# Scores of the second attention by row halves: three products of 64 rows for each head, two heads side by side

## The chip, the cores and the metric

The kernel runs on one core of one Trainium2 chip. The metric is the device time of one execution in microseconds; the time before is the median of three runs. A core has five engines that run their own instruction streams and wait for one another by semaphores: PE (the matrix engine; its weight loads are listed apart as PEld), DVE (the vector engine), ACT (the scalar engine), POOL and SP. PE multiplies a stationary operand (up to 128 rows by 128 columns, loaded first) with a moving operand that streams through, and sums into PSUM; DVE and ACT read PSUM and the on-chip memory SBUF.

## The reference

The model is a two-layer encoder over 512 tokens of width 1024. Layer 0 mixes with RWKV-7 and memory cross-attention, layer 1 with chunked attention against a shared K and V and again memory attention; each layer ends in a convolutional GLU. The part that matters here is the chunked attention of layer 1: twelve heads of 64, queries in chunks of 64, each chunk seeing itself and everything up to eight chunks back, which for 512 tokens is a causal mask by chunks.

```python
def one_chunk(c):
    start = c * CHUNK
    qc = lax.dynamic_slice_in_dim(q, start, CHUNK, axis=2)
    kc = lax.dynamic_slice_in_dim(k_pad, start, BAND, axis=2)
    vc = lax.dynamic_slice_in_dim(v_pad, start, BAND, axis=2)
    s = jnp.einsum('bhqd,bhkd->bhqk', qc, kc).astype(jnp.float32) * scale + bias
    kpos = start - PAD_LEN + jnp.arange(BAND)
    s = jnp.where(kpos >= 0, s, neg)
    p = jax.nn.softmax(s, axis=-1).astype(vc.dtype)
    return jnp.einsum('bhqk,bhkd->bhqd', p, vc)
```

Everything is float32. The kernel keeps that accuracy on PE by splitting each operand into a high part in the matrix engine's rounded type (F32R) and the low rest, `x = h + l`, and summing `h*h + h*l + l*h`.

## The kernel before

The second attention stands between the two feed-forward blocks, inside one `ExitStack` (L1718 onward). The twelve heads go as six pairs; a pair's queries, keys or values are one tile of 128 partitions, head 0 on partitions 0 to 63 (`HS[0]`) and head 1 on 64 to 127 (`HS[1]`). The stage's parts are Python generators:

- `q_proj(i)`, `k_proj(i)`, `v_proj(g)` project. `dense` (L250) makes 24 PE products of 512 columns for one tile (L258, L259, L262), `v_proj` 96 products of 256 columns for two pairs (L1805 to L1807). Their weights are loaded and split by `load_w`: a cast on ACT (L208) and a subtraction on DVE (L216).
- `q_split` (L1763) scales the queries on DVE (L1765) and lays them out per head as a **stack** of 128 partitions: in `qs[:, h]` the head's own 64 partitions hold its high part and the other 64 its low part. That takes a cast on ACT (L1769) and a subtraction on DVE (L1770) per head, each over 64 partitions that may lie elsewhere than their source.
- `k_proj` scales the keys (L1780) and makes two tiles, `ks` (the high part of head h on both halves, L1784 and L1785 on ACT) and `kl` (the low part on both halves, L1787 on DVE): four casts and four subtractions over 64 x 512.
- `attention(i)` runs a pair. `rows(hh, qt)` makes the scores of one head for 128 queries and n = 128 (qt + 1) keys by two products of 128 rows (L1827 with `ks`, L1828 with `kl`): the stack sums all the cross terms inside the array, with the low-by-low term besides. Then come the bias and the row maximum on DVE (L1832), the exponential on ACT (L1834), the reciprocal (L1835) and the scaling on DVE (L1836). `turn(hh, qt)` transposes the result on PE in blocks of 128 (L1842) and copies it to `ptT` on ACT (L1844). The eight units (four query blocks by two heads) go in turn, and a unit is transposed after `LAG = 3` further units have had their scores. At the end L1856 multiplies by the values (64 output columns per head), and the result is put aside or split for the output projection.
- The memory attention of the layer (`mem_qk`, `score_b`, L1908 and L1909) uses the same stacked form and is not changed; its queries come from `q_proj` with a name `"m0"` or `"m1"` as `unit`.

Two chains of generators are merged by `weave` (L99): the attentions with the memory attention between the second and third pair, and the projections with the start of the output projection. Every `yield` carries a cost in ns; `weave` always continues the chain that has used the smaller share of its declared total (`ATT_COST`, L1866, for one pair). Conditions such as `after_unit` hold a projection back until an earlier pair is done, since `ks` and `kl` have two buffers, `qs` three, `sb` four, and the PSUM pool of the stage six banks (two more for `dense`). The tile layer then gives every engine its own fixed order, which follows the merged order but may move an instruction past others; the engine works through that order strictly.

Of the kernel before, what the change touches and what calls it, by code (L numbers as in the profile page):

```python
# [18 lines left out]
P = 128  # L19
# [114 lines left out]
def trunk_kernel(ctx, tc, A, out):  # L134
# [1589 lines left out]
    with ExitStack() as bctx:  # L1724
# [38 lines left out]
        def q_split(ps, T):  # L1763
# [4 lines left out]
            for h in range(2):  # L1768
# [4 lines left out]
        def k_proj(i, T, ps=None):  # L1773
# [7 lines left out]
            ks = ap_.tile([P, 2, S], F32R, name="ks", tag="ks")  # L1781
            kl = ap_.tile([P, 2, S], F32R, name="kl", tag="kl")
            for h in range(2):
                SC.copy(ks[HS[h], h], k_[HS[h]])  # L1784
                SC.copy(ks[HS[1 - h], h], k_[HS[h]])  # L1785
                for rows_ in HS:
                    V.tensor_tensor(kl[rows_, h], k_[HS[h]], ks[HS[h], h], op=ALU.subtract)  # L1787
            T["k"] = ks, kl
# [22 lines left out]
        def attention(i, T):  # L1811
            yield lambda: "k" in T and i // 2 in vS
            qs, (ks, kl) = T["q"], T["k"]
# [7 lines left out]
            def rows(hh, qt):  # L1821
                n = (qt + 1) * P
                st = ap_.tile([P, 4], F32, name="st", tag="st", bufs=6)
# [3 lines left out]
                PE.matmul(ps[:, :n], qs[:, hh, qc], mix(ks[:, hh, :n]), start=True, stop=False)  # L1827
                PE.matmul(ps[:, :n], qs[:, hh, qc], mix(kl[:, hh, :n]), start=False, stop=True)  # L1828
                yield n * 0.94
                sb = sbs[hh, qt] = ap_.tile([P, S], F32, name="sb", tag="sb", bufs=4)  # L1830

                V.tensor_tensor_reduce(flat_(sb[:, :n]), sorted_(ps[:, :n]), flat_(big[hh][:, S - n:S]), -1.0, 3e38,  # L1832
                                       op0=ALU.add, op1=ALU.min, accum_out=st[:, 0:1])
                SC.activation(sb[:, :n], sb[:, :n], AF.Exp, scale=-1.0, bias=st[:, 0:1], accum_out=st[:, 1:2])  # L1834
                V.reciprocal(st[:, 2:3], st[:, 1:2])  # L1835
                V.tensor_scalar(sb[:, :n], sb[:, :n], st[:, 2:3], None, op0=ALU.mult)  # L1836

            def turn(hh, qt):
                n = (qt + 1) * P
                pst_ = ps_s()  # L1840
# [235 lines left out]
```

## Time and profile before

| | |
|---|---|
| time, median of 3 runs | 1252.66 us (1251.97 to 1254.84) |
| time of the profiled execution | 1255.45 us |
| its span, first to last instruction | 1253.7 us |
| granted TensorE clock | 0.998 |
| PE, DVE, ACT busy over the span | 97%, 82%, 67% |
| second attention, 724 to 894 us: PE, DVE, ACT busy | 163.5, 116.9, 116.7 of 170 us |

The span is 1.75 us shorter than the profiled execution's time. "Busy" is the time in which an instruction is listed as running. On PE neighbouring products overlap in the list: a product is shown for its whole passage through the array, while the next one starts as soon as the columns have been streamed in. So the distance from start to start is the price of a product, and a busy PE can still have lost time. The waits view names what an idle engine waited for; the timeline merges neighbours of one kind (x16 is sixteen of them) and gives the idle time before a row in brackets with what ended it.

### The profile page before, as it was taken

The numbers are of one execution on the slowest core, as the hardware profiler recorded it, in microseconds if no ns is written. First come the engines' busy times: TensorE is split into PE (matmuls) and PEld (weight loads), VectorE is DVE, ScalarE is ACT, GpSimd is POOL, SyncE is SP. The second block draws the span as 40 slices with busy tenths as digits, with TensorE's granted clock in tenths as the row PEclk, the third lists the DMA queues.
The fourth block names the chain that finished last, engine by engine and source line by source line (L and its number), as shares of the span: only waits on it lengthen the run. The fifth ranks groups of instructions, "written<-read, shape, count | busy, mean of one in ns | idle before, by whom it ended". The sixth has DMA issues, their size and how long they took to land.

```text
span 1253.7 us, 26444 instructions
## 1 busy us (share of the span) xinstructions
PE 1219.9 (97%) x10420; PEld 1074.8 (86%) x10420; DVE 1027.6 (82%) x1958; ACT 840.5 (67%) x1396; POOL 150.8 (12%) x180
## 2 busy tenths in 40 slices
PE   8999999999999999999999999999999999999997
PEld 6787777777789999999888878777799999998886
DVE  7976677766679999999886976668799999999785
ACT  6557668765567777776664676767667777765662
POOL 1000000000001223221120000000002222221300
PEclk9999999999999999999999999999999999999999
DMA  6356354354063999995995332234428999978961
GB/s 210 97 170 131 82 116 96 80 110 104 19 202 92 205 207 217 208 201 140 307 223 144 99 113 68 85 109 135 130 56 189 206 214 212 202 167 259 257 169 67
DMA packets 95293, 191.10 MB, mean 152 GB/s; under 512 B 22080, under 2 KB 30400, under 8 KB 95168
## 3 DMA queue, kind: packets, MB, share of 16 engines
q1 hardware_dynamic: 68592, 129.14, 32.3%
q0 software_dynamic: 26576, 60.26, 27.7%
q8 instruction: 82, 1.34, 0.4%
q14 instruction: 43, 0.35, 0.1%
HBM read 173.15 MB, written 6.29 MB: 143 GB/s over the span
## 4 chain that ended last, share of the span: by engine, by line
PE 66%; DVE 14%; ACT 8%; DMA 7%; issue 4%; POOL 0%; SPq 0%; DVEq 0%; ACTq 0%; POOLq 0%
PE psf L453 11%; PE psf L735 7%; PE psf L455 6%; PE psf L461 4%; PE psd L262 4%; PE psd L258 4%; PE psd L259 4%; PE psf L740 4%; PE psd L735 3%; PE psf L466 2%; DVE wlo L216 2%; PE psd L740 2%; DMA tmp<-r2h 1%; DMA tmp<-r1h 1%; PE pss L1856 1%
## 5 line engine op out<-in xcount | busy, mean ns | idle before, releaser
L529 ACT CAST whi<-raw 128x1024 fp32r<-128x1024 f32 (+1 forms) x168 | 150.3, 937 | 22.6 <-PE psf L453 19.6
L208 ACT CAST whi<-wraw 128x1024 fp32r<-128x1024 f32 x84 | 87.3, 1045 | 63.7 <-PE psd L259 33.9
L453 PE MATMUL psf<-tl,whi 128*128 128x256 f32 x512 | 121.5, 275 | 0.1
L453 PE MATMUL psf<-th,whi 128*128 128x256 f32 x512 | 121.3, 276 | 0.0
L534 DVE TENSOR_TENSOR wlo<-raw,whi 128x1024 fp32r<-128x1024 f32 (+1 forms) x108 | 108.9, 1010 | 0.0
L258 PE MATMUL psd<-r1h,whi 128*128 128x512 f32 x264 | 104.1, 395 | 0.0
L259 PE MATMUL psd<-r1l,whi 128*128 128x512 f32 x264 | 101.7, 386 | 0.0
L453 PEld LDWEIGHTS psf<-tl,whi 128*128 128x128 f32 x512 | 98.4, 192 | 0.5 <-DVE tl L276 0.5
L453 PEld LDWEIGHTS psf<-th,whi 128*128 128x128 f32 x512 | 98.2, 192 | 0.1
L216 DVE TENSOR_TENSOR wlo<-wraw,whi 128x1024 fp32r<-128x1024 f32 x67 | 81.6, 1218 | 19.0 <-ACT whi L208 18.5
L725 ACT CAST whi<-raw 128x1024 fp32r<-128x1024 f32 (+1 forms) x52 | 49.4, 950 | 51.1 <-PE psf L735 27.4
L726 DVE TENSOR_TENSOR wlo<-raw,whi 128x1024 fp32r<-128x1024 f32 (+1 forms) x52 | 56.4, 1096 | 28.3 <-ACT whi L725 24.9
L501 POOL DMA_DIRECT2D wlv<-in_ffn_in_dram x40 | 48.2, 1204 | 250.7 <-ACT wlv L500 187.5
L455 PE MATMUL psf<-th,wlo 128*128 128x256 f32 x504 | 77.1, 276 | 0.0
L556 ACT ACTIVATE tmp<-tmp,vec 128x512 f32<-128x512 f32 x44 | 36.0, 818 | 58.2 <-DVE tmp L543 58.2
L262 PE MATMUL psd<-r1h,wlo 128*128 128x512 f32 x264 | 70.3, 389 | 0.0
L455 PEld LDWEIGHTS psf<-th,wlo 128*128 128x128 f32 x504 | 66.4, 192 | 0.0
L258 PEld LDWEIGHTS psd<-r1h,whi 128*128 128x128 f32 x264 | 49.8, 189 | 9.1 <-issue 2.0
L259 PEld LDWEIGHTS psd<-r1l,whi 128*128 128x128 f32 x264 | 49.9, 189 | 6.4 <-issue 0.7
L262 PEld LDWEIGHTS psd<-r1h,wlo 128*128 128x128 f32 x264 | 47.9, 189 | 6.8 <-issue 0.3
L516 DVE TENSOR_TENSOR raw<-raw 128x1024 f32<-128x1024 f32 x42 | 51.1, 1217 | 0.0
L258 PE MATMUL psd<-r2h,whi 128*128 128x512 f32 x128 | 50.3, 394 | 0.5 <-ACT r2h L1706 0.3
(622 smaller groups left out, 3741.1 us busy)
## 6 DMA issues: line engine op xcount, KB each, us to landing
raw<-in_ffn_in_dram SPq DMA_DIRECT2D x42, 512.0 KB, 5.1
raw<-in_ffn_in_dram SPq DMA_DIRECT2D x84, 256.0 KB, 5.6
wlv<-in_ffn_in_dram POOLq DMA_DIRECT2D x40, 512.0 KB, 7.7
raw<-in_ffn_out_dram SPq DMA_DIRECT2D x30, 512.0 KB, 6.3
raw<-in_ffn_out_dram POOLq DMA_DIRECT2D x24, 512.0 KB, 9.9
wraw<-in_wA_dram SPq DMA_DIRECT2D x20, 512.0 KB, 4.1
wraw<-in_w_out_dram SPq DMA_DIRECT2D x16, 512.0 KB, 4.2
wraw<-in_ffn_outp_dram SPq DMA_DIRECT2D x16, 512.0 KB, 5.6
```

Of the source, the lines that this page charges most:

```text
L208: high = lambda: pin(SC.copy(hi[:, :n], raw))
L216: pin(V.tensor_tensor(lo[:, :n], raw, hi[:, :n], op=ALU.subtract))
L258: PE.matmul(ps, wh[:, j * P:(j + 1) * P], ah, start=start and n == 0, stop=False)
L259: dense_at[0] = PE.matmul(ps, wh[:, j * P:(j + 1) * P], al, start=False, stop=False)
L262: dense_at[0] = PE.matmul(ps, wl[:, j * P:(j + 1) * P], moving(act(k))[0], start=False, stop=stop and n == len(ks) - 1)
L453: PE.matmul(ps, wh[:, o + k * P:o + k * P + P], x[k][n], start=k == n == 0, stop=False)
L455: PE.matmul(ps, wl[:, ol + k * P:ol + k * P + P], x[k][0], start=False, stop=k == 3)
L529: keep(SC.copy(hi[:, :n], self.pair(what) if n > S else self.raw[:, what]))
L534: keep(V.tensor_tensor(lo[:, :n], self.pair(what) if n > S else self.raw[:, what], hi[:, :n], op=ALU.subtract))
L726: V.tensor_tensor(lo, s_, hi, op=ALU.subtract)
L735: PE.matmul(ps[:], a[:, k0 + i, ts], woven(hi[:, i * S:i * S + S]), start=bool(first) and (first is True or t in first) and a is act[0] an ...
L740: PE.matmul(ps[:], act[0][:, k0 + i, ts], woven(lo[:, i * S:i * S + S]), start=False, stop=bool(last) and t in last and i == n - 1)
```

## The change

Queries and keys of the six attention pairs are no longer stacked. `split_to` (L274: one ACT cast, one DVE subtraction, over all 128 partitions) writes the high parts of both heads into `qs[:, 0]` and `ks[:, 0]`, the low parts into `qs[:, 1]` and `ks[:, 1]`; each head stays on its own 64 partitions. `kl` goes from this path. The stacked branch stays for the memory attention.

The scores of a head are now three products that use only the head's 64 rows: high by high, high by low, low by high. `rows(qt)` handles both heads: the loop over the parts is outside and the heads alternate inside, each head summing into a PSUM bank of its own. `turn(qt)` transposes both heads, and a query block is transposed after the next block's scores. The yields and `ATT_COST` change with that.

```diff
+        PARTS = (0, 0), (0, 1), (1, 0)
...
-            q_split(ps, T)
+            q_split(ps, T, unit is not None)
...
+            if not stacked:
+                split_to(qs[:, 0], qs[:, 1], q[:])
+            for h in range(2) if stacked else ():
                 SC.copy(qs[HS[h], h], q[HS[h]])
                 V.tensor_tensor(qs[HS[1 - h], h], q[HS[h]], qs[HS[h], h], op=ALU.subtract)
...
-            ks = ap_.tile([P, 2, S], F32R, name="ks", tag="ks")
-            kl = ap_.tile([P, 2, S], F32R, name="kl", tag="kl")
-            for h in range(2):
-                SC.copy(ks[HS[h], h], k_[HS[h]])
-                SC.copy(ks[HS[1 - h], h], k_[HS[h]])
-                for rows_ in HS:
-                    V.tensor_tensor(kl[rows_, h], k_[HS[h]], ks[HS[h], h], op=ALU.subtract)
-            T["k"] = ks, kl
+            ks = T["k"] = ap_.tile([P, 2, S], F32R, name="ks", tag="ks")
+            split_to(ks[:, 0], ks[:, 1], k_[:])
...
-            def rows(hh, qt):
+            def rows(qt):
...
-                ps = ps_s()
-                qc = slice(qt * P, (qt + 1) * P)
-                PE.matmul(ps[:, :n], qs[:, hh, qc], mix(ks[:, hh, :n]), start=True, stop=False)
-                PE.matmul(ps[:, :n], qs[:, hh, qc], mix(kl[:, hh, :n]), start=False, stop=True)
-                yield n * 0.94
+                pss = [ps_s() for _ in range(2)]
+                for a, b in PARTS:
+                    for hh, ps in enumerate(pss):
+                        PE.matmul(ps[:, :n], qs[HS[hh], a, qc], mix(ks[HS[hh], b, :n]), start=a == b, stop=a == 1)
+                yield 2 * n * 0.7
...
-            us = [(hh, qt) for qt in range(4) for hh in range(2)]
-            for n, u in enumerate(us):
-                yield from rows(*u)
-                if n >= LAG:
-                    yield from turn(*us[n - LAG])
-            for u in us[-LAG:]:
-                yield from turn(*u)
+            for qt in range(4):
+                yield from rows(qt)
+                if qt >= 1:
+                    yield from turn(qt - 1)
+            for qt in range(4 - 1, 4):
+                yield from turn(qt)
...
-        ATT_COST = 2 * 1280 * 1.7 + 2300
+        ATT_COST = 2 * 1280 * 1.47 + 2300
```

How this changes the fixed orders is seen at two places. The first is PE at the start of the last pair, behind the value products of the pair before (L1856); `pss<-ks,qs` and `pss<-kl,qs` are scores, `pss<-cst,sb` transposes, `psd` rows belong to the output projection. Before:

```order
L1856 MATMUL pss<-ptT,vS 64x128 x2
L1827 MATMUL pss<-ks,qs 128x128
L1828 MATMUL pss<-kl,qs 128x128
...
L1842 MATMUL pss<-cst,sb 128x128
L1827 MATMUL pss<-ks,qs 128x384
L1828 MATMUL pss<-kl,qs 128x384
L262 MATMUL psd<-r2h,wlo 128x512 x4
L258 MATMUL psd<-r2h,whi 128x512
L1842 MATMUL pss<-cst,sb 128x128
L1827 MATMUL pss<-ks,qs 128x384
L1828 MATMUL pss<-kl,qs 128x384
L1842 MATMUL pss<-cst,sb 128x128 x2
```

And with the change:

```order
L1856 MATMUL pss<-ptT,vS 64x128 x2
L1826 MATMUL pss<-ks,qs 128x128 x6
L1826 MATMUL pss<-ks,qs 128x256 x6
L259 MATMUL psd<-r2l,whi 128x512
L262 MATMUL psd<-r2h,wlo 128x512 x4
L1842 MATMUL pss<-cst,sb 128x128
L262 MATMUL psd<-r2h,wlo 128x512 x2
L1842 MATMUL pss<-cst,sb 128x128
L1826 MATMUL pss<-ks,qs 128x384 x6
L1842 MATMUL pss<-cst,sb 128x128 x4
L1826 MATMUL pss<-ks,qs 128x512 x6
```

The two heads' scores of a query block now stand together as one group of six, and the transposes of the second block's two heads stand together right behind the third block's scores.

The second place is ACT where the keys of the fourth pair are split while the third pair's last blocks are copied out of PSUM. Before:

```order
L1834 ACTIVATE sb,st<-sb,st 128x512
L1844 COPY ptT<-pss 128x3x128
L1784 CAST ks<-tmp 64x512
L1785 CAST ks<-tmp 64x512
L1784 CAST ks<-tmp 64x512
L1785 CAST ks<-tmp 64x512
L1844 COPY ptT<-pss 128x4x128 x2
```

With the change:

```order
L208 CAST whi<-wraw 128x1024
L1833 ACTIVATE sb,st<-sb,st 128x512 x2
L1845 COPY ptT<-pss 128x3x128 x2
L275 CAST ks<-tmp 128x512
L1845 COPY ptT<-pss 128x4x128 x2
```

Ahead of the last two copies, for which the value products wait, there is one cast in the place of four.

More of the change, by code (lines that the diff above doesn't have):

```diff
@@ L1819, in attention @@
             sbs = {}
[L1821 removed]
+            def rows(qt):
                 n = (qt + 1) * P
[L1823 removed]
+                qc = slice(qt * P, (qt + 1) * P)
                 mix, flat_, sorted_ = (woven, halved, plain_order) if qt > 1 else (lambda t: t,) * 3
[L1825 to L1836 removed]
@@ new lines, in turn @@
+            def turn(qt):
+                n = (qt + 1) * P
+                psts = [ps_s() for _ in range(2)]
+                for hh, pst_ in enumerate(psts):
+                    for kt in range(qt + 1):
+                        PE.transpose(pst_[:, kt * P:(kt + 1) * P], sbs[hh, qt][:, kt * P:(kt + 1) * P], C("ident"))
+                yield 2 * n * 0.85
+                for hh, pst_ in enumerate(psts):
+                    SC.copy(pts[hh][:, 0:qt + 1, qt * P:(qt + 1) * P], pst_[:, :n].rearrange("p (a b) -> p a b", b=P))
```

19 lines of the change are left out of this document (10 added, 9 removed).

## The prediction

> **What bounds the kernel now.** First the page: the slices of the span, and the chain that ended last.
>
> ```profile
> PE   8999999999999999999999999999999999999997
> PE 66%; DVE 14%; ACT 8%; DMA 7%; issue 4%; POOL 0%; SPq 0%; DVEq 0%; ACTq 0%; POOLq 0%
> ```
>
> PE is busy in every slice and holds two thirds of the chain. So a microsecond of matrix work added or taken away on PE counts in full, while one on DVE or ACT counts only where PE waits for it. The table by stretches, over the second attention cut by its pairs (first and fifth stretch, and the sum of all seven):
>
> ```profile
> 724.00:754.00 30.00, 27.65 (x185) 23.36 (x184) 23.44 (x56) 22.45 (x49) 0.29 (x2) 1.00 0.32 96
> 826.00:846.00 20.00, 19.39 (x144) 16.49 (x142) 9.77 (x34) 12.02 (x31) 0.33 (x2) 1.00 0.27 93
> sum 170.00, PE 163.51 PEld 130.68 DVE 116.86 ACT 116.67 POOL 1.45; mean PE 23.36 PEld 18.67 DVE 16.69 ACT 16.67 POOL 0.21
> ```
>
> In 170 us PE is idle for 6.5, while DVE and ACT have 53 us to spare each. What PE waits for in 724 to 905 us, from the waits view (total, times, longest):
>
> ```profile
> PE pss L1842 <- DVE st L1835: 1.5, 2, 0.9
> PE pss L1856 <- ACT ptT L1844: 1.4, 3, 0.5
> PE pss L1827 <- ACT ks L1785: 1.1, 2, 0.6
> PE pss L1842 <- DVE sb L1836: 0.7, 3, 0.2
> ```
>
> So PE waits for the softmax (L1842), for the copies ahead of the value products (L1856) and for the split keys (L1827). These waits cap what less work on DVE and ACT can return.
>
> **The change, part by part.** *Less streaming.* Full-array scores from the timeline (start, listed duration):
>
> ```profile
> 757.29 0.27 PE L1828 MATMUL pss<-kl,qs 128*128 128x128 f32 x1
> 757.40 0.33 PE L1827 MATMUL pss<-ks,qs 128*128 128x256 f32 x1
> 757.57 0.28 PE L1828 MATMUL pss<-kl,qs 128*128 128x256 f32 x1
> 757.68 0.38 PE L258 MATMUL psd<-r2h,whi 128*128 128x512 f32 x1
> ...
> 741.25 0.33 PE L1828 MATMUL pss<-kl,qs 128*128 128x384 f32 x1
> 741.41 0.38 PE L258 MATMUL psd<-r1h,whi 128*128 128x512 f32 x1
> ...
> 742.07 0.44 PE L1842 MATMUL pss<-cst,sb 128*128 128x128 f32 x2
> 742.26 0.46 PE L1827 MATMUL pss<-ks,qs 128*128 128x512 f32 x1
> 742.56 0.38 PE L1828 MATMUL pss<-kl,qs 128*128 128x512 f32 x1
> 742.77 0.81 PE L262 MATMUL psd<-r1h,wlo 128*128 128x512 f32 x3
> ```
>
> From start to start a product of 128 columns takes 0.11 us, of 256 0.11, of 384 0.16, of 512 0.21: 0.60 for one product in each of the four query blocks (0.11 + 0.11 + 0.16 + 0.215). A pair made four such sets (two heads, two products), 2.4 us; if the halves run side by side it makes three, 1.8. Six pairs: **-3.6 us**. Do the halves run side by side? No F32R product on 64 rows stands in this trace, but plain f32 ones do: in the first layer L1338 alternates the two halves into two banks, and L1628 stays on one half for a run.
>
> ```profile
> 307.57 1.99 PE L1628 MATMUL pss<-kmT,kn 64*128 64x256 f32 x8
> 85.27 0.38 PE L258 MATMUL psd<-r1h,whi 128*128 128x512 f32 x1
> 85.49 0.38 PE L259 MATMUL psd<-r1l,whi 128*128 128x512 f32 x1
> 85.80 0.60 PE L1338 MATMUL pss<-AR,KB 64*128 64x128 f32 x6
> 85.80 1.16 PE L1338 MATMUL pss<-AR,KB 64*128 64x128 f32 x16
> 86.89 0.48 PE L258 MATMUL psd<-r1h,whi 128*128 128x512 f32 x1
> 87.21 0.38 PE L259 MATMUL psd<-r1l,whi 128*128 128x512 f32 x1
> ```
>
> The run's sixth product of L1338 ends 0.60 after its start and the sixteenth 1.16: five pairs in 0.56, 0.112 a pair. On one half alone, L1628's eight products of 256 columns take 1.99, at most 0.25 each, 0.12 for 128 columns. So a pair costs what one product costs: the halves overlap. These operands stream at about half the F32R pace (512 columns in 0.21 above); that the overlap holds at the full pace is carried over, not seen.
>
> *A switch on each side.* The same rows give the price of leaving the full array and coming back. From 85.49 to 87.21 are 1.72 us: the slots of L259 and L258 (0.216 each, by 85.27 to 85.49) and eight pairs at 0.112 make 1.33. The rest, **0.39 us**, is the switch in and out. Before the change no score pays it: in 742.07 to 742.56 two transposes at 0.11 and a score at 0.215 make 0.435 of the 0.49. In the changed order the scores stand in 24 separate groups (five in the first pair, three in the second, then four, five, four, three, with one or more full-array rows between): 24 x 0.39 = **+9.4 us**. One group follows the value products, whose 64 columns already left the full mode: -0.2. Together with the streaming PE's own work grows by 5.6 us. The bounds: 24 switches of nothing (-3.6), and the switch in full with no overlap of the halves, in which case six products stand where four stood (+3.6 in the place of -3.6), at +12.8.
>
> The Trainium skill speaks against the change too: TensorEngine Tiling, Key Properties, says that a change of the tiling mode, not just of the tile, drains the engine. It gives no price; with none the sum would keep the -3.6, with the rows' 0.39 it is as above.
>
> *Less splitting.* The groups of 724 to 894 us:
>
> ```profile
> L1787 DVE TENSOR_TENSOR kl<-tmp,ks 64x512 fp32r<-64x512 f32 x24 | 16.4, 684 | 0.4
> L1770 DVE TENSOR_TENSOR qs<-tmp,qs 64x512 fp32r<-64x512 f32 x16 | 11.0, 686 | 0.5
> L1769 ACT CAST qs<-tmp 64x512 fp32r<-64x512 f32 x16 | 9.9, 618 | 5.6 <-DVE tmp L1765 5.3
> L1784 ACT CAST ks<-tmp 64x512 fp32r<-64x512 f32 x12 | 7.4, 617 | 2.1 <-DVE tmp L1780 2.0
> ```
>
> Twelve query casts become six (the four for the memory queries stay), 24 key casts become six; the subtractions likewise. A cast over 128 partitions is taken at the same 0.62 us as over 64, as its columns are the same (the bounds are nothing and twice that, which moves a part of the next term). That is 24 x 0.617 = 14.8 us off ACT and 24 x 0.685 = 16.4 off DVE, all beside PE. It pays where PE waited behind these casts. At the start of the stage and ahead of the second pair's value products:
>
> ```profile
> 728.37 0.28 PE L1807 MATMUL pss<-wlo,r1h 128*128 128x256 f32 x1
> 729.25 0.33 PE L1827 MATMUL pss<-ks,qs 128*128 128x128 f32 x1 [0.60 <-ACT ks L1785]
> 729.68 0.38 PE L259 MATMUL psd<-r1l,whi 128*128 128x512 f32 x1
> 730.53 0.33 PE L1827 MATMUL pss<-ks,qs 128*128 128x128 f32 x1 [0.47 <-ACT ks L1785]
> 731.03 0.38 PE L1805 MATMUL pss<-whi,r1h 128*128 128x256 f32 x1 [0.17 <-ACT vS L1809]
> ...
> 749.10 0.38 PE L258 MATMUL psd<-r2h,whi 128*128 128x512 f32 x1
> 750.02 1.12 PE L1856 MATMUL pss<-ptT,vS 128*64 128x512 f32 x3 [0.54 <-ACT ptT L1844]
> ```
>
> Start to start, less the slot of the product ahead, the first place loses 0.77 + 0.63 + 0.39 = 1.8 us. Five of the first ten casts there go, and 71 value products now stand ahead of the first score, not 48: I take all of the 1.8. At 749.10 the loss is 0.92 - 0.215 = 0.70 for 0.54 of listed idle, so a listed wait costs 0.16 more than it shows; the three waits of L1856 cost 1.4 + 3 x 0.16 = 1.9, and three casts less (1.85 us) ahead of those copies cover each of them. Smaller delays of the fourth and fifth pair's keys I put at 0.8. **-4.5 us**; bounds: nothing, and all 6.5 of idle with its 0.16 for each of some 16 waits, -9.
>
> *Heads in step.* The second block's transposes of both heads now follow the third block's scores directly in four pairs, with a little dense work between in two. How late the second head was, in the first pair:
>
> ```profile
> 740.51 0.30 PE L1842 MATMUL pss<-cst,sb 128*128 128x128 f32 x1 [0.57 <-DVE st L1835]
> 742.46 0.35 DVE L1836 TENSOR_SCALAR sb<-sb,st 128x256 f32<-128x256 f32 x1
> ```
>
> Its scaled block was ready at 742.81, 2.3 us after the first transpose. In the new order PE is there after two transposes (0.22), two dense products (0.43) and the 384-column group (0.48 + 0.39): 1.5 us, and waits 0.8. Behind the waiting transposes stand the 512-column scores, and DVE and ACT wait for those. Six times up to 0.8, less what the freed DVE and ACT bring forward: I take **+2.0** (0 to 4.8). Against it, where PE waits for the first block's softmax anyhow (the L1842 rows), the way out of the new group runs inside the wait: 0.2 in each pair, **-1.3** (0 to -2.4).
>
> Sum: 5.6 - 4.5 + 2.0 - 1.3 = **+1.8 us**. The profiled execution took 1255.45 for a span of 1253.7, 2.8 above the median; the term is a difference, so I put it on the median, 1252.66: **1254.5 us**.
>
> **The rivals.**
>
> *The paired transposes wait.* One mechanism, at the transposes of the second block behind the 384-column scores: the full 4.8 us of waits and, PE being late anyway, nothing of the switches hidden: 5.6 - 4.5 + 4.8 = +5.9, 1258.6. It decides from 1.4 us of such waits on (5.6 - 4.5 + 1.4 = 2.5). For it speaks that the lag is shorter by one head and that DVE serves the two heads one after the other; against it, DVE and ACT are each freed of about 9% of the stage.
>
> *The lighter engines win.* PE's waits all but vanish (-9) and the lag costs nothing (0), the switch staying as priced: 5.6 - 9 = -3.4, 1249.3. For it: the longest single waits are behind casts that go. Against it: the two largest left are L1842 behind the softmax's own steps, which stay.
>
> *No overlap at full pace.* The banks or the array take the two F32R streams one after the other: 5.6 + 7.2 - 4.5 + 0.7 = +9.0, 1261.7. The rows above show the overlap at half pace only.
>
> *Loads do not hide.* With three products per half and a new load for each, every pair shows its load. An exposed load is seen in 742.26 to 742.56, 0.30 for a slot of 0.215: 0.085. With 72 pairs this adds 6.1, +7.9, 1260.6. Against it: L1338's pairs, each with its own load, run at 0.112 without a gap. This is the Trainium skill's rule in TensorE: Matmul & The Clock Gate, The mechanism, by which a load overlaps a running product only when the row group differs; the trace disagrees for the f32 pairs.
>
> **How the numbers follow.** About 0.2% (2.5 us) is what a measurement of this kernel can tell from no change. The forecast, within that of the median: 0.40. The paired transposes wait 0.26, no overlap 0.07, loads do not hide 0.05: slower 0.38. The lighter engines win: faster 0.22. The forecast's own range is 1251 to 1257; for 8 in 10 it reaches down past the faster case's 1249.3, and up through the loads' 1260.6 to the no-overlap case: 1248.5 to 1261.5.
>
> **What would show it.** The new score line runs in pairs a few ns apart, 0.215 us a pair at 512 columns; if 0.43, the halves do not overlap. The product ahead of a group and the first behind it stand about 0.39 further apart than the slots between. PE's waits on L1785 are gone and those of the value products on the ptT copies short; the waits of the transposes on L1836's successor are longer. PE's idle time in the stage falls while its busy time rises by about 5 us. The forecast is wrong if a group costs under 0.2 us of switching, or if the transposes' waits fall as well.

## The result, and the profile after

The changed kernel is slower, by about 4 us. It was compared with the kernel before on two occasions, with these medians:

| comparison | with the change | before | ratio, 95% interval |
|---|---|---|---|
| first | 1259.05 us (8 runs, 1256.37 to 1262.19) | 1254.27 us (8 runs) | 1.0030 (1.0015 to 1.0044) |
| again, with the experiments below | 1259.06 us (12 runs) | 1255.58 us (35 runs) | 1.0032 (1.0016 to 1.0048) |

The ratios are those of the record; the quotient of the two medians is 1.0038 and 1.0028. The time lies inside the predicted range of 1248.5 to 1261.5, but the likeliest case, no change at 1254.5, is not what came. The profiled execution took 1257.51 us with a span of 1255.7, against 1255.45 and 1253.7 before: 2.0 us apart.

The attention itself is the first place to look. The chain of the page, then the table by stretches of the changed kernel (columns as before: window, length, PE busy, PEld, DVE, ACT, POOL, granted clock, DMA share, GB/s):

```profile
PE 65%; DVE 15%; ACT 8%; DMA 7%; issue 5%; POOL 0%; SPq 0%; DVEq 0%; ACTq 0%; POOLq 0%
```

```profile
724.00:754.00 30.00, 28.98 (x196) 23.40 (x195) 18.12 (x48) 18.53 (x42) 0.29 (x2) 1.00 0.29 94
826.00:846.00 20.00, 19.61 (x142) 15.96 (x142) 9.85 (x34) 11.06 (x30) 0.29 (x2) 1.00 0.27 93
sum 170.00, PE 164.28 PEld 128.35 DVE 102.58 ACT 101.64 POOL 1.31; mean PE 23.47 PEld 18.34 DVE 14.65 ACT 14.52 POOL 0.19
```

DVE and ACT have lost 14.3 and 15.0 us of work, where 16.4 and 14.8 had been computed. PE is listed as busy for 0.8 us more. What PE waits for in 724 to 905 us:

```profile
PE pss L1842 <- DVE st L1834: 3.2, 5, 1.4
PE pss L1842 <- DVE sb L1835: 1.8, 6, 0.4
PE pss L1803 <- ACT vS L1807: 0.7, 2, 0.5
```

The waits for split keys and those of the value products are gone, and those of the transposes (L1842) for the softmax on DVE have grown from 2.2 to 5.0 us. From PE's first product of the stage's norm (L328) to the first product of the projection's third output tile (the first `psf` row of L258) the kernel before took 177.76 us and the changed one 177.83. So the attention came out even, and the two microseconds are lost later. PE's waits in 893 to 965 us, before and after:

```profile
PE psf L453 <- ACT whi L529: 0.7, 2, 0.4
```

```profile
PE psf L453 <- ACT whi L529: 1.4, 2, 1.0
PE psf L453 <- DVE r1l L317: 0.8, 2, 0.4
PE psf L453 <- ACT r1h L316: 0.5, 1, 0.5
```

These are the first products of the second feed-forward (L453). They now wait for `r1h` and `r1l`, the split of its input. ACT's timeline shows why those are late (in brackets the idle time before a row and what ended it); first before, then with the change:

```profile
908.31 0.70 ACT L887 ACTIVATE tmp<-xT,vec 128x512 f32<-128x512 f32 x1
908.92 1.03 ACT L208 CAST whi<-wraw 128x1024 fp32r<-128x1024 f32 x1
911.17 1.04 ACT L275 CAST th<-sp 128x1024 fp32r<-128x1024 f32 x1 [1.22 <-DVE sp L898]
```

```profile
907.50 0.72 ACT L887 ACTIVATE tmp<-xT,vec 128x512 f32<-128x512 f32 x1
912.74 1.05 ACT L208 CAST whi<-wraw 128x1024 fp32r<-128x1024 f32 x1 [4.52 <-DMA wraw<-in_w_out_dram]
913.69 1.04 ACT L275 CAST th<-sp 128x1024 fp32r<-128x1024 f32 x1
```

ACT stands still for 4.5 us, because the projection's last weight has not landed, and everything behind its cast in ACT's order, the cast to `th` (L275) and the next splits of the input, is later by 2.5 us. The weight is late, to begin with, because it was asked for late. The issues of the three last weight loads on SP, before and after (start, length of the row, count of issues in it):

```profile
895.83 2.06 SPq L227 DMA_DIRECT2D wraw<-in_w_out_dram  x2
902.68 0.33 SPq L227 DMA_DIRECT2D wraw<-in_w_out_dram  x1
```

```profile
895.04 0.33 SPq L227 DMA_DIRECT2D wraw<-in_w_out_dram  x1
901.81 4.21 SPq L227 DMA_DIRECT2D wraw<-in_w_out_dram  x2
```

A load needs a free buffer, and the buffer of the second of the three came free later, because the subtraction that reads it (L216, the split of the projection's fifth weight) went further back in DVE's order. The last load then waits for the sixth weight's subtraction, which comes behind it on DVE. Before, the fifth weight's subtraction follows the sum into `xT` of the second output tile (L426); now it follows that of the third:

```profile
895.72 0.68 DVE L426 TENSOR_TENSOR xT<-xT,psd 128x512 f32<-128x512 f32 x1
896.32 1.22 DVE L216 TENSOR_TENSOR wlo<-wraw,whi 128x1024 fp32r<-128x1024 f32 x1
```

```profile
899.93 0.68 DVE L426 TENSOR_TENSOR xT<-xT,psf 128x512 f32<-128x512 f32 x1
900.53 1.22 DVE L216 TENSOR_TENSOR wlo<-wraw,whi 128x1024 fp32r<-128x1024 f32 x1
```

This makes the request for the last weight 3.0 us later in the timeline (905.69 for 902.68). The load then also takes twice as long to land: 7.0 us (at 912.66) for 3.5 before (at 906.15). Before, it was asked for ahead of two loads that POOL issues; now it comes behind them. Their rows, before and after:

```profile
904.91 1.74 POOL L496 DMA_DIRECT2D tmp<-in_ffn_in_dram  x2 [31.93 <-PE psf L262]
```

```profile
904.15 1.75 POOL L496 DMA_DIRECT2D tmp<-in_ffn_in_dram  x2 [32.88 <-DVE r1l L317]
```

In the changed kernel the second of these lands at 912.48, just ahead of the weight. In the four profiles whose last weight is asked for within 1.6 us of the second POOL load, it takes 5.9 to 7.0 us; in the seven that ask 2.5 to 3.3 us behind it, 4.0 to 5.2. So about half of its lateness is this meeting of loads; that they share the DMA engines is the likely reason, and no run isolates it.

Neither L426 nor L216 is part of the change. The tile layer gives every engine its order for the whole program, and this place came out differently.

### The profile page after: what moved, and what is told of

It is laid out like the page before. It is cut to its first block, busy times and chain, and to the rows that moved or that the text cites. A ratio compares the mean times of both kernels' runs of the same rounds, so it can differ in the third digit from the quotient of the medians.

```text
span 1255.7 us, 26482 instructions
## 1 busy us (share of the span) xinstructions
PE 1221.3 (97%) x10468; PEld 1072.5 (85%) x10468; DVE 1013.1 (81%) x1934; ACT 825.4 (66%) x1372; POOL 150.7 (12%) x180
## 4 chain that ended last, share of the span: by engine, by line
PE 65%; DVE 15%; ACT 8%; DMA 7%; issue 5%; POOL 0%; SPq 0%; DVEq 0%; ACTq 0%; POOLq 0%
PE psf L453 11%; PE psf L735 7%; PE psf L455 6%; PE psf L461 5%; PE psd L258 4%; PE psf L740 3%; PE psd L262 3%; PE psd L259 3%; PE psd L735 3%; PE psf L466 2%; DVE wlo L216 2%; PE psd L740 2%; DMA tmp<-r1h 1%; DMA raw<-in_ffn_in_dram 1%; PE pss L1856 1%
## 5 line engine op out<-in xcount | busy, mean ns | idle before, releaser
L208 ACT CAST whi<-wraw 128x1024 fp32r<-128x1024 f32 x84 | 87.4, 1045 | 73.6 <-PE psd L259 36.8
L453 PE MATMUL psf<-tl,whi 128*128 128x256 f32 x512 | 121.5, 275 | 0.1
L453 PE MATMUL psf<-th,whi 128*128 128x256 f32 x512 | 121.3, 276 | 0.0
L258 PE MATMUL psd<-r1h,whi 128*128 128x512 f32 x264 | 104.7, 397 | 0.0
L216 DVE TENSOR_TENSOR wlo<-wraw,whi 128x1024 fp32r<-128x1024 f32 x67 | 81.7, 1220 | 22.6 <-ACT whi L208 21.1
L453 PEld LDWEIGHTS psf<-tl,whi 128*128 128x128 f32 x512 | 98.3, 192 | 0.5 <-DVE tl L276 0.5
L453 PEld LDWEIGHTS psf<-th,whi 128*128 128x128 f32 x512 | 98.1, 192 | 0.1
L258 PEld LDWEIGHTS psd<-r1h,whi 128*128 128x128 f32 x264 | 49.9, 189 | 9.9 <-issue 2.4
L258 PE MATMUL psd<-r2h,whi 128*128 128x512 f32 x128 | 50.2, 392 | 0.3 <-ACT r2h L1706 0.3
```

Of the source, the lines that this page charges most:

```text
L208: high = lambda: pin(SC.copy(hi[:, :n], raw))
L216: pin(V.tensor_tensor(lo[:, :n], raw, hi[:, :n], op=ALU.subtract))
L258: PE.matmul(ps, wh[:, j * P:(j + 1) * P], ah, start=start and n == 0, stop=False)
L453: PE.matmul(ps, wh[:, o + k * P:o + k * P + P], x[k][n], start=k == n == 0, stop=False)
```

## The experiments

Two theories. *Order at the projection*: the attention is even, and the loss comes from the order that the planner gave to the weights' splits behind it. *Switches*: the loss is PE's own work in the attention. Each kernel has a profile; from each come two lengths that repeat well: the stage as above, and the time from the first to the hundred-and-first product of L453 in the second feed-forward. The rest of the program, the same in all of them, does not repeat as well: the stretch ahead of the stage ended between 714.1 and 718.7 us in the ten profiles of the experiments, without any edit there.

| kernel | stage, us | first hundred of L453, us | time against before, 95% interval |
|---|---|---|---|
| before | 177.76 | 21.69 | |
| the change | 177.83 | 24.33 | 1.0030 (1.0015 to 1.0044) |
| the change again | 177.85 | 24.45 | 1.0032 (1.0016 to 1.0048) |
| early split | 177.92 | 22.14 | 0.9998 (0.9988 to 1.0009) |
| before, late split | 179.59 | 22.40 | 1.0005 (0.9991 to 1.0019) |
| before, late split and late cast | 179.57 | 24.14 | 1.0021 (1.0006 to 1.0036) |
| early split, no alternation | 178.74 | 22.25 | 1.0022 (1.0006 to 1.0037) |
| early split, full rows | 168.11 | 21.63 | 0.9914 (0.9890 to 0.9939) |
| early split, two groups | 177.48 | 22.38 | 0.9982 (0.9969 to 0.9995) |
| the same, more between | 177.89 | 22.03 | 0.9994 (0.9980 to 1.0008) |
| early split, splits put back | 183.36 | 22.87 | 1.0035 (1.0019 to 1.0051) |
| before, heads in step | 177.67 | 21.66 | 0.9992 (0.9978 to 1.0007) |

In the two late variants of the kernel before, 1.6 us of the stage are not theirs: the granted clock fell for a moment (last section).

### The changed kernel with the split early

Only `out_proj` of the second layer differs: the fourth and fifth weight are loaded and split right behind the first two sums, and the two steps of the feed-forward's input behind them are held until the fifth weight's subtraction (`low_at`) has been issued. PE's order is the same as the changed kernel's, row by row.

```diff
+            if m < len(own):
+                ws[m + 3] = load_w(A["w_out"][l, m + 3])
+            with tc.issue_after(low_at[0].ins) if own and m == 1 else ExitStack():
+                for _ in range((0, 2)[m] if m < len(own) else 1):
+                    next(taken)
-            next(taken)
```

> The changed kernel, in which only the order around the output projection of the second layer is another: the fifth weight of the projection is split on DVE (L216) right behind the sum into xT of the second output tile, where the kernel before has it, and not behind the sum of the third. PE's order is the same. Theory 'late weight': the attention itself came out even (PE at the first product L258 of the third output tile at 894.37 before, 894.23 after), and the loss arises because this split is 4.2 us later, which delays the load behind it, then an ACT cast, then the splits of x at the start of the feed-forward. Then the profiled span falls by the 2.0 us of the profiles, to about 1253.7, the 4.5 us wait of ACT for a weight at 912 us and PE's waits for r1h and r1l at 925 to 930 us go, and the time comes back to within 0.2% of the kernel before. Rival 'switches': the loss is that of PE's own work in the attention, and the time stays about 4 us above the kernel before.

Measured: 1256.50 us (12 runs) against 1256.63 (29 runs), 0.9998 (0.9988 to 1.0009). On ACT the last weight's cast now waits 1.2 us, and PE's waits for `r1h` and `r1l` are gone:

```profile
911.41 1.05 ACT L275 CAST th<-sp 128x1024 fp32r<-128x1024 f32 x1 [1.55 <-DVE sp L898]
913.62 1.04 ACT L208 CAST whi<-wraw 128x1024 fp32r<-128x1024 f32 x1 [1.16 <-DMA wraw<-in_w_out_dram]
```

```profile
PE psf L453 <- ACT whi L529: 1.9, 2, 1.1
```

The first hundred products of L453 take 22.14 us, 2.2 less than with the change. The span of this one profile is 1256.4 and did not fall as expected, since the stretches outside scatter by more than that (the stage began at 717.87, not 716.40); the medians did what the theory says. With this order, the change is a change of nothing.

The reason is not the one that was expected. The last weight does not come earlier here: it is asked for at 909.13 and lands at 913.55, which is 17.8 us behind the end of the stage, for 18.4 with the change and 11.8 before. But the edit has also put its cast behind the cast to `th`, as the rows show, and so ACT does not hold `th` back while it waits. In the kernel before and in the changed one the last weight's cast comes first. So two things make the loss together: a last weight that lands late, and a cast of it that stands ahead of the one to `th`. The kernel before has only the second, and the early split only the first.

### The kernel before with the split late

```diff
+        def late_w(src):
+            hi, lo, second = split_w(raw_w(src), 1024, hold=True)
+            with tc.issue_after(add.ins):
+                second()
+            return hi, lo
...
-                nxt = load_w(A["w_out"][l, m + 1]) if m + 1 < KD else None
+                nxt = (late_w if l and m == 3 else load_w)(A["w_out"][l, m + 1]) if m + 1 < KD else None
```

(`add` is the sum into `xT` of the tile before.)

> The kernel before, in which only the split of the fifth weight of the output projection is put behind the sum of the third output tile on DVE, as it stands in the changed kernel; the attention is untouched. 'Late weight': 2 to 4 us slower than the kernel before, ACT waits some 4 us for a weight at about 910 us and PE waits for r1h and r1l at the start of the feed-forward. 'Switches': no change.

Measured: 1256.94 us against 1256.63, 1.0005 (0.9991 to 1.0019): no change, where 2 to 4 us were expected. The load was late as in the changed kernel, but it cost the first hundred of L453 only 0.7 us. So a late split does not cost the loss by itself. The rows show why. Here, too, the cast to `th` stands ahead of the last weight's cast in ACT's order, though the edit did not ask for it, and ACT uses the wait for it:

```profile
914.53 1.05 ACT L275 CAST th<-sp 128x1024 fp32r<-128x1024 f32 x1 [1.39 <-DVE sp L898]
917.63 1.04 ACT L208 CAST whi<-wraw 128x1024 fp32r<-128x1024 f32 x1 [2.05 <-DMA wraw<-in_w_out_dram]
```

### The kernel before with the late split and the late cast

The same, and the second split of the token sums is held until the last weight's cast (`high_at`) has been issued; for that the last weight's load stands earlier in the program. ACT's order is then that of the kernel before again, where the last weight's cast comes first as well (908.92 and 911.17 above):

```diff
+            if l and m == 4:
+                w7 = load_w(A["w_out"][l, 7])
+                with tc.issue_after(high_at[0].ins):
+                    held_th[0]()
             next(taken)
...
-                    split_to(*(t[:, m - 1:m + 1].rearrange("p a s -> p (a s)") for t in (Th, Tl)), su)
+                    th = [t[:, m - 1:m + 1].rearrange("p a s -> p (a s)") for t in (Th, Tl)]
+                    held_th[0] = lambda h=th, u=su: split_to(*h, u)
+                    if l == 0 or m != 3:
+                        held_th[0]()
```

> The kernel before with two things of the changed kernel's order around the projection and nothing of its attention: the fifth weight's split stands late on DVE, and on ACT the cast of the last weight stands ahead of the second split of the token sums (the cast to th, L275), as it does in the changed kernel. 'Order at the projection, both together': the first hundred products of the second feed-forward take 24.3 us as in the changed kernel, not 21.7, and the time rises by 2 to 4 us. If that order is not the cause, no change (0.9991 to 1.0019 with the late split alone).

Measured: 1260.26 us against 1256.77, 1.0021 (1.0006 to 1.0036). ACT's wait is there, in a kernel whose attention nobody touched:

```profile
917.88 1.04 ACT L208 CAST whi<-wraw 128x1024 fp32r<-128x1024 f32 x1 [5.70 <-DMA wraw<-in_w_out_dram]
918.83 1.04 ACT L275 CAST th<-sp 128x1024 fp32r<-128x1024 f32 x1
```

The first hundred of L453 (L457 in this kernel) take 24.14 us, as in the changed kernel. The waits in them are not the same ones: PE waits mostly for the casts of the feed-forward's weights on ACT (1.7 us) and little for `r1l` (0.2), and PE's own order came out another there. A further 1.5 us are lost inside the projection, where PE waits for a weight's split (1.3 us, `whi` of L208); the changed kernel does not lose those.

The time of this kernel is weaker evidence than its lengths. Nine of its twelve runs had a mean granted clock of 0.997 or less; the three at 0.998 or more took 1254.90 to 1257.21 us, in the mean 1256.0, and the kernel before took 1256.1 at such clocks (8 runs). So for the time the cause rests on the early split: another order of the projection takes the loss of the changed kernel away, with PE's order the same. The lengths show it both ways: with a late weight the first hundred take 24.1 to 24.5 us when its cast comes first (the change twice, and this kernel) and 22.1 to 22.4 when it comes second (the early split and the late split); the kernel before has the cast first and the weight in time, 21.7.

### The change again

The kernel of the change, unedited.

> The changed kernel as it is, once more, timed beside the kernel before on the chip of the following runs. 'Order at the projection' (the loss is made at the start of the feed-forward by where the weights' splits came to stand, since the same kernel with the early split measured 0.9998 of the kernel before): again slower by 2 to 5 us, and the profile shows again some 4 us of ACT waiting for a weight near 912 us and 2 to 3 us of PE waits behind 925 us. 'Scatter' (the first comparison was unlucky, and the change was even all along): within 1 us of the kernel before.

Measured: 1.0032 (1.0016 to 1.0048). The first comparison was not unlucky, and the loss does not hang on the clock: in the runs with a mean granted clock of 0.998 or more the change took 1257.8 us (7 runs) and the kernel before 1254.4 (13 runs). ACT's wait is there again, 4.48 us, and so are PE's for `r1l` and `r1h` (1.1 and 0.5):

```profile
910.96 1.05 ACT L208 CAST whi<-wraw 128x1024 fp32r<-128x1024 f32 x1 [4.48 <-DMA wraw<-in_w_out_dram]
```

### Without alternation

On the kernel of the early split, as are the next four.

```diff
-                for a, b in PARTS:
-                    for hh, ps in enumerate(pss):
+                for hh, ps in enumerate(pss):
+                    for a, b in PARTS:
```

> The kernel of the early split, in which the three score products of head 0 stand one behind the other and then the three of head 1: no alternation of the row halves. If the halves overlap at the full pace only when they alternate, a group of scores streams up to five sets where the alternating one streams three: 2 x 0.60 us for each of six pairs, 7.2 us more of PE's own work than with the early split, some of it inside waits: 5 to 8 us slower. If the overlap is worth nothing, no change.

Measured: 1258.44 us against 1256.63, 1.0022 (1.0006 to 1.0037), about 3 us above the early split by the ratios (2 by the medians), where 5 to 8 were expected; the stage is 0.8 us longer. The compiled program has the three products of head 0 and then the three of head 1, and PE does not run them so. A group of six at 512 columns, in PE's timeline of the changed kernel and of this one:

```profile
741.81 0.38 PE L259 MATMUL psd<-r1l,whi 128*128 128x512 f32 x1
742.12 0.92 PE L1826 MATMUL pss<-ks,qs 64*128 64x512 f32 x6
742.96 1.56 PE L262 MATMUL psd<-r1h,wlo 128*128 128x512 f32 x6
```

```profile
740.98 0.38 PE L259 MATMUL psd<-r1l,whi 128*128 128x512 f32 x1
741.29 0.92 PE L1826 MATMUL pss<-ks,qs 64*128 64x512 f32 x6
742.14 0.70 PE L262 MATMUL psd<-r1h,wlo 128*128 128x512 f32 x2
```

The group takes 0.84 us and 0.85 us to the next product. One after the other, with only the third product of head 0 beside the first of head 1, it would be five times 0.216, 1.08, and the switch. The six starts lie in pairs, 3 ns apart with alternation (742.440 and 742.442, then 742.656 and 742.658 in the changed kernel) and 10 ns apart without (741.286 and 741.296, 741.606 and 741.616, 741.822 and 741.832). The rows do not name the half, but the semaphores do: the first two products each wait for their bank, and the last two each report theirs done. So a pair is one product of each head, and the halves overlap whichever way the products stand in the program. Whether more than the stage's 0.8 us is lost is not shown: the intervals of this kernel and of the early split overlap.

### Full rows

```diff
-                for a, b in PARTS:
-                    for hh, ps in enumerate(pss):
-                        PE.matmul(ps[:, :n], qs[HS[hh], a, qc], mix(ks[HS[hh], b, :n]), start=a == b, stop=a == 1)
+                for u, (a, b) in enumerate(PARTS):
+                    ps = pss[u % 2]
+                    PE.matmul(ps[:, :n], qs[:, a, qc], mix(ks[:, b, :n]), start=u < 2, stop=u > 0)
```

> The kernel of the early split, in which each group of scores is three products over all 128 rows in the place of three pairs over 64: the same streaming, but no switch of the array. It leaves out the separation of the heads (the scores of both are summed together, and two of the three parts go to the first head's bank). If a group costs 0.39 us of switching, PE's own work falls by 24 x 0.39 = 9.4 us, less 0.2; what of it was inside PE's waits comes back as waits, up to 2.4 us: 6 to 9 us faster than the early split. If a switch costs nothing, no change.

Measured: 1244.05 us (4 runs) against 1256.63, 0.9914 (0.9890 to 0.9939), 10.6 us below the early split by the ratios and 9.8 in the stage, where 6 to 9 were expected. Over the stage, the slots of at most 0.33 us above their price by columns shrink by 5.9 us, 0.25 for each of 24 groups (a full-array group keeps edges of its own), and the longer waits by 3.6: the transposes' waits fall too, which was not expected. The planner placed some of the transposes later in this kernel, so the second part is not the switches' alone.

```profile
PE pss L1842 <- DVE st L1834: 1.3, 3, 0.7
PE pss L1842 <- DVE sb L1835: 0.3, 1, 0.3
```

### Two groups instead of four

`rows` takes several blocks, makes all their scores, then their softmax.

```diff
-            for qt in range(4):
-                yield from rows(qt)
-                if qt >= 1:
-                    yield from turn(qt - 1)
-            for qt in range(4 - 1, 4):
-                yield from turn(qt)
+            for g in [rows(0, 1), turn(0), rows(2, 3), turn(1), turn(2), turn(3)]:
+                yield from g
```

> The kernel of the early split, in which the scores of the first two query blocks stand as one group and those of the last two as another: 13 groups in the place of 24. By the changed kernel's trace a group costs PE 0.29 us of switching (0.10 on the way in, 0.10 inside, 0.10 on the way out): 11 groups less are 3.2 us, by the prediction's 0.39 they are 4.3. If PE's own work decides, 3 to 4 us faster than the early split, so faster than the kernel before; if the transposes' waits take it back (the second block's two heads now stand behind two blocks of scores, and the softmax of four units comes at once), no change or slower, with L1842's successor waiting 3 us or more longer in total.

Measured: 1253.95 us against 1255.58, 0.9982 (0.9969 to 0.9995), below the kernel before and the lowest but for the kernel that leaves the separation of the heads out. In the stage, the short slots give back 3.45 us, 0.35 for each of ten groups (the built program has 14 groups, not the 13 that were expected), between the two prices of the expectation; the longer waits take 3.1 of them again:

```profile
PE pss L1847 <- DVE st L1839: 4.5, 4, 1.4
PE pss L1847 <- DVE sb L1840: 2.7, 4, 0.8
```

The stage is 0.4 us shorter than with the early split. That is less than the 0.16% between the ratios, whose intervals overlap, so the gain over the kernel before is small, if it is one.

### More work between scores and transposes

```diff
-                yield sum(2 * (qt + 1) * P * 0.7 for qt in qts)
+                yield sum(2 * (qt + 1) * P * 1.3 for qt in qts)
...
-                yield 2 * n * 0.85
+                yield 2 * n * 0.55
...
-        ATT_COST = 2 * 1280 * 1.47 + 2300
+        ATT_COST = 2 * 1280 * 1.8 + 2300
```

> The kernel of the two groups, in which the weaving gives the projections more of their work right behind a pair's scores (the cost given for a block's scores is 1.3 per column in the place of 0.7, that of its transposes 0.55 in the place of 0.85, and a pair's total goes with them). The order of the last two pairs is the same. If the waits of the transposes for the softmax (7.2 us in 12 waits with two groups) come from too little work behind the scores, they shrink in the first four pairs, by 1 to 3 us of the time; if the softmax chain on DVE itself is late, they only move to later transposes: no change.

Measured: 0.9994 (0.9980 to 1.0008), no gain. The transposes' waits fell from 7.2 to 5.5 us, and waits for the values' copies rose from 1.3 to 2.6: moved, not taken away.

### Splits put back

```diff
             if not stacked:
+                x = ap_.tile([P, 2, S], F32R, name="kl", tag="kl")
+                SC.copy(x[HS[0], 0], q[HS[0]])
+                V.tensor_tensor(x[HS[0], 1], q[HS[0]], x[HS[0], 0], op=ALU.subtract)
                 split_to(qs[:, 0], qs[:, 1], q[:])
...
+            for r, c in ((HS[0], 0), (HS[1], 0), (HS[0], 1)):
+                SC.copy(x[r, c], k_[r])
+                V.tensor_tensor(x[r, c], k_[r], x[r, c], op=ALU.subtract)
             split_to(ks[:, 0], ks[:, 1], k_[:])
```

> The kernel of the early split, with as many casts and subtractions over 64 x 512 put back ahead of the keys' and queries' splits as the change took away (one of each for a query tile, three of each for a key tile, written to a tile that nothing reads). The prediction's step 'less splitting' says 4.5 us slower than the early split, with bounds of nothing and 9. If the casts lay beside PE for nothing, no change.

Measured: 1.0035 (1.0019 to 1.0051), 4.6 us above the early split; the stage is 5.4 us longer. The waits for keys are back:

```profile
PE pss L1833 <- ACT ks L275: 1.3, 2, 1.0
PE pss L1863 <- ACT ptT L1852: 0.7, 1, 0.7
```

### Heads in step, nothing else

The kernel before with its stacked scores and its splits, and with the early split's edit in the projection; `rows(qt)` and `turn(qt)` as in the change, with this in the middle:

```diff
+                for hh, ps in enumerate(pss):
+                    PE.matmul(ps[:, :n], qs[:, hh, qc], mix(ks[:, hh, :n]), start=True, stop=False)
+                    PE.matmul(ps[:, :n], qs[:, hh, qc], mix(kl[:, hh, :n]), start=False, stop=True)
+                yield 2 * n * 0.94
```

> The kernel before with its stacked full-array scores and its splitting, in which only the heads step together as in the changed kernel (both heads' scores of a block, then the transposes of the block before); the projection has the order with the early split. The prediction's step 'heads in step' says 2.0 us slower than the kernel before, from longer waits of the transposes of the second block (0 to 4.8); if the longer waits only take the place of others, no change.

Measured: 0.9992 (0.9978 to 1.0007); the stage is 177.67 us. No loss, so not the 2.0 us. The transposes' waits for DVE are 2.8 us here, 0.6 more than before:

```profile
PE pss L1844 <- DVE st L1836: 1.9, 4, 0.9
PE pss L1844 <- DVE sb L1837: 0.9, 3, 0.4
```

## Why the prediction was right or wrong

The prediction summed the attention stage to +1.8 us and called the whole kernel no change. The stage measured +0.07. The kernel is slower by what happens behind it, which is no term of the sum. That is the step that failed: "the term is a difference, so I put it on the median" took for granted that work outside the stage keeps its order. The compiled order of the change says otherwise, in DVE's rows around L426 and L216, and the last weight lands 6.5 us later in front of a cast that the feed-forward needs; the prediction looked at the two orders only at the places that the diff speaks of.

Within the stage, the table compares the terms. It is worked out from the starts of all PE products: the distance from a product to the next, less the price of its columns (0.216 us for 512 of F32R, 0.16 for 384, 0.109 for 256 or fewer and for a transpose). The value products are those of the memory attention too, which the change leaves alone and which give 1.0 of the 2.3.

| term | predicted | before | change | difference |
|---|---|---|---|---|
| streaming of the scores | -3.6 | 14.3 | 11.1 | -3.3 |
| short slots ahead of, in and behind the scores | +9.2 | 1.6 | 7.0 | +5.3 |
| long waits ahead of or behind scores, and ahead of value products | in the -4.5 | 4.7 | 0.4 | -4.4 |
| the value products themselves | in the -4.5 | 19.9 | 17.6 | -2.3 |
| ahead of transposes | +2.0 and -1.3 | 4.6 | 7.7 | +3.1 |
| other | 0 | | | +1.5 |
| sum | +1.8 | | | +0.07 (each row is rounded by itself) |

*Less streaming* was right. The halves overlap at the full F32R pace: a pair of 512 columns takes 0.216 us, and the loads are hidden but for the first pair behind a switch. *No overlap* and *Loads do not hide* fall. With the latter falls the rule that the prediction took from the Trainium skill (TensorE: Matmul & The Clock Gate, The mechanism) that a load overlaps a running product only when the row group differs: in the trace of the early split, the last load of a half starts at 741.801, while the product of the same half that started at 741.798 still streams, and the product that it is for starts at 741.961, 0.163 behind that product, the bare price of 384 columns. The same section of the Trainium skill also lets a load into the background weight buffer go ahead of running products; the trace does not tell the buffer.

*A switch on each side* had the right mechanism and nearly the right price; what it missed is what the stacked scores paid. The Trainium skill states a drain at each change of the tiling mode (TensorEngine Tiling, Key Properties). The trace agrees as far as each group loses time at its edges, and prices it. In the rows above, 741.81 to 742.12 is 0.31 for a slot of 0.216, and 742.12 to 742.96 is 0.84 for three pairs of 0.216: together 0.29 us a group. Where two dense or value projection products follow a group, the first of them takes 0.10 too long as well (742.964 to 743.284 is 0.320). That makes the 0.39 that the prediction had from L1338. Eighteen of the 24 groups are followed so; these slots cost 1.9 us in the change, and the same slots behind stacked scores 0.5 before. The difference of 1.35 is most of the 1.5 under other. So the groups cost 7.0 and 1.9, together 8.9 us, for the 9.2 of the prediction. But the stacked scores had been taken to pay nothing, while their own edges cost 1.6 and 0.5. So the term is +5.3 and 1.35, about +6.7. Taking ten groups away gives 0.35 each, and replacing all 24 by full-array groups 0.25 each, which agrees.

*Less splitting* was right in size: putting the casts back cost 4.6 us of time and 5.4 in the stage, for the 4.5 predicted. In the change itself it gave more, 6.7 with the value products (1.0 of it in the memory attention), which no longer wait for the second head's copy in their midst. That part needs the fewer casts: heads in step with all the casts leave the value products at 19.3 us, in the kernel with the splits put back as in the one with the heads in step alone. Fewer casts without the step were not tried.

*Heads in step* was too low in the change (+3.1 for +0.7) and too high alone (no loss). The rival *The paired transposes wait* was to decide from 1.4 us on; the transposes' waits grew by more than that, and it still did not decide, as it held the other terms fixed while two of them came out better. Its time, 1258.6, is close to the measured 1259.05 for another reason. *The lighter engines win* fell with the transposes' waits. That the stage came out within 2 us of its sum is luck in part: the switches came out 2.5 below their term, the splitting gave 2.2 more, and the heads in step cost 2.4 more.

Of "what would show it", the pairs, the vanished waits on keys and the longer waits on the softmax came as written. The first product behind a group stands 0.29 further from the one ahead of it, not 0.39, which the second one does. PE's busy time rose by 0.8 us, not 5.

What stays open is the size behind the stage: the profiles of the change show 2.6 to 2.8 us there, and the two comparisons 3.8 and 4.0 (intervals from 1.9 to 6.0). Why the planner chose another order is argued only: it places instructions by a clock of its own, and the stage ahead of the projection ended at another time on that clock.

## What to carry to other kernels

Where a planner orders the whole program, compare the orders over the whole program, behind the change above all, and look for weight splits, casts and loads that moved: where an engine takes its instructions in order, as ACT did in its 4.5 us, one late load stops everything behind its consumer. Count a switch of the array by its group, with what the old form paid at its own edges, and put products that need it together only as far as their consumers keep up. A gain on engines beside the bound one can be real (4.6 us here) and still be needed in full to pay for the rest.

## What the runs showed of the hardware

The halves of the array need no alternating program. With three products of one half ahead of three of the other, the starts still came in pairs, 10 ns apart instead of 3, in the same 0.85 us. The Trainium skill (TensorE: Matmul & The Clock Gate, The mechanism) says that products start strictly in the order of the program, without reordering; this trace disagrees for F32R products on different row halves, where the first product of the second head starts 0.31 us ahead of the second product of the first. So what was said ahead of the prediction, that an engine works through its order strictly, is too strong for PE.

The granted clock can fall for a few microseconds in the middle of a stage. In both late variants of the kernel before, fifteen or so value projections (256 columns) ran at 0.213 us in the place of 0.112, from one product to the next; the window's clock shows it, in the first of them and then in the second (the trace has a grant of one half for 3.4 us):

```profile
732.00:738.00 6.00, 5.36 (x30) 4.91 (x29) 2.38 (x4) 1.65 (x5) 0.00 (x0) 0.72 0.00 0
```

```profile
731.00:737.00 6.00, 5.47 (x32) 5.33 (x33) 1.98 (x3) 1.61 (x4) 0.00 (x0) 0.72 0.00 0
```

That is 1.6 us of stage, with a mean clock of 0.995 and 0.996 over these two executions, and may be one reason why single spans of the same program differ by more than the effects told of here.
